# A streaming encoder step: the sample group's cache loads on ScalarE's queue, and small transfers merged

## The chip, the cores and the metric

The kernel runs on one core of a Trainium2 chip. The metric is the time of one execution on the device, in microseconds (us). Engines: PE is TensorE, DVE is VectorE, ACT is ScalarE, POOL is GpSimd, SP is SyncE, which computes nothing and only starts transfers. All transfers are carried by the core's 16 DMA engines.

## What is computed

One layer of an encoder, for two groups of requests that share the weights. The prompt group is one stream of 2048 new frames; the sample group is 8 streams of 16 new frames, each with 1024 cached frames. All numbers are float32. For both groups:

```
h = rmsnorm(x) * (1 + scale) + shift
z = h @ w_in                       # two conv parts, q, k, v, f
attention: s = q.k / 8 + cum_q - cum_k (causal), p = softmax(s), out = p.v
x = x + g1 * (concat(conv_module, attention) @ w_out)
x = x + g2 * ((silu(h2 @ w_gate) * (h2 @ w_up)) @ w_down)
```

`cum` is the running sum of the log forget values of a head. For a sample stream the keys, values and forget values are the cached ones followed by the new ones: `cache_k`, `cache_v` (8 streams, 1024 frames, 8 heads of 64) and `cache_logf`.

## The kernel before

The program goes through four stages: the projections (to about 625 us), the attention (625 to 1190 us), the output projection and the feed-forward part (the rest). The change lies in the attention.

**The prompt's attention** (`attention`, `attend`, from L804) is cut into 16 steps: a pair of heads `p` and a block `qb` of 512 queries. A step goes over tiles of 128 keys; for each tile and head PE makes a score tile (L1035, L1041, L1043) in one of three PSUM banks, ACT takes its exponential (L1045), PE multiplies by the values (L999). The row maxima come from products of their own (L952), which DVE reduces (L957), some 32 to 48 score tiles ahead; the maxima of a step are then written as a row, `mrow` (L970), into the query operand by eight transfers of 0.5 KB (L972). At the end of a step (`end_of_step`, L1062) the sums of the exponentials, four rows (two in a step with `qb` = 0) at partitions 0, 32, 64 and 96 of `sm`, are written to DRAM (L1080), loaded back in another shape (L1084), inverted on DVE (L1089), written (L1090), and loaded as a tile `aR` in which each of two rows is repeated over 64 partitions (L1094); DVE multiplies the result `zc` by it (L1097). These pieces are issued 3, 8, 13 and 20 score tiles after the end of the step (L1100).

**The sample's attention** runs as a background beside it (`background`, L878, woven in by `weave`). From `sample_setup` (L1135) on it holds the cached keys of a stream in two tiles `kc` of 1 MB (three buffers), the cached values in two tiles `vc` of 1 MB (two buffers), and the bias in a tile `S` (two buffers). `S` of stream `b` + 2 is loaded in the middle of `sample_values(b)` (L1305), the values of `b` + 1 after its products (L1315), and the keys three tiles ahead, after every second pair of key products (L1265). The bias stands in DRAM as four arrays `bias_d[j]` (rows: stream, head; 256 columns) and `biasn_d` (16 columns). Each row is repeated over the 16 queries of a stream, which makes 8 + 2 transfers for a stream (L1218, L1222), because head 2g + h stands in row 8s + 2g + h while the tile wants the halves h apart.

**The order of the work.** The engines take their instructions in a fixed order that the framework draws up at compile time, by the order of the program, priorities (the background's are 100 later) and a model of times. `late` and `after` add edges of order alone. All of these transfers are issued by SP, in its one order. The compiled program gives the transfers of the hardware queues eight semaphores in turn, and a transfer is held back by its issuing engine until the one eight places before it has landed.

```
1265  self.next_keys(2 * b + c + 3)
1266  yield
...
1315  self.next_values_of(b + 1)
1316  yield
```

Of the kernel before, what the change touches and what calls it, by code (L numbers as in the profile page):

```python
# [11 lines left out]
ALU = mybir.AluOpType  # L12
# [4 lines left out]
P = 128  # L17
# [3 lines left out]
NTP = T // P  # L21
NT = NTP + 1
TT = NT * P
NS = 8
QS = 16
H = 8
HD = 64
NP = H // 2
PAST = 1024
# [98 lines left out]
class Layer:  # L128
# [933 lines left out]
    def end_of_step(self, p, qb, zc, sums):  # L1062


        nc, wk = self.nc, self.awk
        parts = 2 if qb else 1
        r = slice(0, 64 * parts)
        sm = wk.tile([P, 512], F32, tag="sm", name="sm", bufs=1)
        self.last_exp = nc.scalar.copy(sm[r], sums[r])
        cat = self.cat_d[:, 4 + p, qb * 512:(qb + 1) * 512]  # L1070
        R = wk.tile([P, 512], F32, tag="R", name="aR", bufs=1)
        if (p, qb) == STEPS[-1]:
            spread = self.bank("ss", "R")
            nc.tensor.matmul(spread, self.four, sm, start=True, stop=True)
            nc.vector.reciprocal(R, spread)
            nc.vector.tensor_tensor(zc, zc, R, ALU.mult)
            nc.gpsimd.dma_start(cat, zc)
            return
        for i in range(2 * parts):
            nc.sync.dma_start(self.sum_d[p, qb, i:i + 1], sm[32 * i:32 * i + 1])  # L1080
        w = wk.tile([P, 2, 2, 4], F32, tag="inv", name="inv")

        def load():
            nc.sync.dma_start(w[:, 0:parts], self.sum_d[p, qb, 0:2 * parts].rearrange("(k h) (a c) -> a k h c", h=2, c=4))  # L1084

        def invert():
            if qb:
                self.after(nc.vector.tensor_tensor(w[:, 0], w[:, 0], w[:, 1], ALU.add), self.last_max)
            self.after(nc.vector.reciprocal(w[:, 0], w[:, 0]), self.last_max)  # L1089
            nc.sync.dma_start(self.inv_d[p, qb].rearrange("h (a c) -> a h c", c=4), w[:, 0])  # L1090

        def back():
            for h in range(2):
                nc.sync.dma_start(R[HD * h:HD * h + HD], self.inv_d[p, qb, h:h + 1].broadcast_to([HD, 512]))  # L1094

        def divide():
            self.after(nc.vector.tensor_tensor(zc, zc, R, ALU.mult), self.last_max)  # L1097
            nc.sync.dma_start(cat, zc)

        self.due += [(self.nscore + k, f) for k, f in ((3, load), (8, invert), (13, back), (20, divide))]  # L1100

    def late(self, op, last):
# [32 lines left out]
    def sample_setup(self, bank):  # L1135

        nc, a, sm = self.nc, self.a, self.smp
# [9 lines left out]
        sel = sm.tile([P, NS + QS], F32, name="sel")  # L1147
# [28 lines left out]
        for b in range(2):  # L1176
            pb = bank.rearrange("p (i k) -> p i k", i=4)
            for i in range(4):
# [4 lines left out]
                suf[:n, 4 * b:4 * b + 4].unsqueeze(2).broadcast_to([n, 4, P]), ALU.add)  # L1183
            yield
        lm = sm.tile([P, NS, H], F32, name="lm")
        nc.vector.tensor_tensor(lm, self.logf[:, NTP, :].unsqueeze(1).broadcast_to([P, NS, H]),
                                sel[:, 0:NS].unsqueeze(2).broadcast_to([P, NS, H]), ALU.mult)
        yield
        pn = bank[:, :QS]
        self.pe(pn[:n, :], lm.rearrange("p s h -> p (s h)"), sel[:, NS:], start=True, stop=True)  # L1190
# [10 lines left out]
        yield  # L1201
        yield

    def next_keys(self, i):

        if i < 2 * NS:
            kt = self.smc.tile([P, NP, 512], F32, tag="kc", name="kc", bufs=3)
            self.nc.sync.dma_start(kt, self.a["kcT"][i // 2, :, :, i % 2 * 512:i % 2 * 512 + 512])
            self.kc.append(kt)

    def next_bias(self, b):

        if b < NS:
            S = self.smp.tile([P, PAST + NP * QS], F32, tag="S", name="S", bufs=2)
            for j in range(4):
                for h in range(2):
                    rows = self.bias_d[j].rearrange("(s g h) k -> s h g k", s=NS, h=2)[b, h]
                    self.nc.sync.dma_start(S[32 * j + QS * h:32 * j + QS * h + QS, :PAST].rearrange("p (g k) -> p g k", g=NP),  # L1218
                                           rows.unsqueeze(0).broadcast_to([QS, NP, PAST // 4]))
            for h in range(2):  # L1220
                rows = self.biasn_d.rearrange("(s g h) k -> s h g k", s=NS, h=2)[b, h]
                self.nc.sync.dma_start(S[QS * h:QS * h + QS, PAST:].rearrange("p (g k) -> p g k", g=NP),  # L1222
                                       rows.unsqueeze(0).broadcast_to([QS, NP, QS]))
            kS = self.smp.tile([P, NP, QS], F32, tag="kS", name="kS", bufs=2)
            self.nc.sync.dma_start(kS, self.a["o_k"][:, :, T + b * QS:T + (b + 1) * QS].rearrange("g p t -> p g t"))
            self.S.append((S, kS))

    def next_values_of(self, b):

        if b < NS:  # L1230
            vs = []
            for c in range(2):
                v = self.smc.tile([P, 4, DC], F32, tag="vc", name="vc")
                self.nc.sync.dma_start(v, self.a["vc"][b, c * 512:c * 512 + 512].rearrange("(t p) e -> p t e", p=P))
                vs.append(v)
            vn = self.smp.tile([QS, DC], F32, tag="vn", name="vn")
            self.nc.sync.dma_start(vn, self.a["o_v"][T + b * QS:T + (b + 1) * QS, :])
            self.vs = vs, vn

    def sample_scores(self, b, bank):  # L1240

        S, kS = self.S.pop(0)
        Sc = S[:, :PAST].rearrange("p (g c k) -> p g c k", g=NP, c=2)
        Sn = S[:32, PAST:].rearrange("p (g k) -> p g k", g=NP)

        def q(g):
            return self.Qbd[:, g, b].rearrange("p h q -> p (h q)")

        for g in range(NP):
            self.pe(bank[:32, QS * g:QS * g + QS], q(g), kS[:, g, :], start=True, stop=True, tile_position=(0, 0))  # L1250
        yield
        self.dve("tensor_tensor", Sn, Sn, bank[:32, :NP * QS].rearrange("p (g k) -> p g k", g=NP), ALU.add)
        self.dve("tensor_tensor", Sn, Sn, self.maskS[:32].unsqueeze(1).broadcast_to([32, NP, QS]), ALU.add)
        yield
        for i in range(4):
            c, g0 = i // 2, i % 2 * 2
            if g0 == 0:
                kt = self.kc.pop(0)
            for g in (g0, g0 + 1):
                keys = kt[:, g].rearrange("p (t j k) -> p j t k", j=4, k=32)  # L1260
                for j in range(4):
                    self.pe(bank[32 * j:32 * j + 32, (g - g0) * P:(g - g0) * P + P].rearrange("p (t k) -> p t k", k=32), q(g), keys[:, j],
                            start=True, stop=True, tile_position=(0, 32 * j))
            if g0:
                self.next_keys(2 * b + c + 3)  # L1265
            yield
            s = Sc[:, g0:g0 + 2, c]
            self.dve("tensor_tensor", s, s, bank.rearrange("p (g k) -> p g k", g=2), ALU.add)
            yield
        self.scored = S, Sn  # L1270

    def sample_values(self, b, bank):

        sm = self.smp
        S, Sn = self.scored
# [13 lines left out]
        for g in range(NP):  # L1289
            s = S[:, g * PAST // 4:(g + 1) * PAST // 4]  # L1290
# [6 lines left out]
        parts = sm.tile([P, NP, 32], F32, tag="ob", name="parts")  # L1297
# [10 lines left out]
        for kt in range(9):  # L1308
            for g in range(NP):
                r = slice(32 * g, 32 * g + 32)  # L1310
                e = slice(g * P, (g + 1) * P)
                lhs, rhs = (ST[:, g, kt], vs[kt // 4][:, kt % 4, e]) if kt < 8 else (EnT[:QS, g], vn[:, e])
                self.pe(o[r, :], lhs, rhs, start=(kt == 0), stop=(kt == 8), tile_position=(0, 32 * g))
        self.pe(den, parts.rearrange("p g r -> p (g r)"), self.ones[:, 0:1], start=True, stop=True)
        self.next_values_of(b + 1)  # L1315
        yield
        ob = sm.tile([P, P], F32, tag="ob", name="ob")
        rd = sm.tile([P, 1], F32, tag="rd", name="rd")
        self.dve("reciprocal", rd, den)
# [466 lines left out]
def host_layout(inp):  # L1786
    import numpy as np

    inp = {n: np.asarray(v) for n, v in inp.items()}

    def c(x):
        return np.ascontiguousarray(x)
# [5 lines left out]
    def cols(w):  # L1798
# [21 lines left out]
        "w_down": c(inp["w_down"][0].reshape(NF // 2, 2, P, CB, P).transpose(1, 3, 2, 0, 4)),  # L1820
        "kcT": c(inp["cache_k"][0].reshape(NS, PAST, NP, P).transpose(0, 3, 2, 1)),
        "vc": c(inp["cache_v"][0].reshape(NS, PAST, DC)),
        "clfT": c(inp["cache_logf"][0].reshape(NS, 8, P, H).transpose(2, 1, 0, 3).reshape(P, 8, NS * H)),
        "ident": np.eye(P, dtype=np.float32),
    }
    i = np.arange(P)
# [8 lines left out]
    g = i % 32 // 8  # L1835
# [39 lines left out]
```

## Time and profile before

| | us |
|---|---|
| median of 3 runs (2797.23 to 2807.96) | 2799.87 |
| the profiled execution | 2804.1 |
| its span, first to last instruction | 2802.3 |
| PE busy in the span | 2716.7 |
| ACT busy in the span | 1235.4 |
| mean granted TensorE clock | 0.984 of full |

All durations below are of the profiled execution. A line such as L1045 is a line of the kernel. "SPq" is SP as the issuer of transfers, "DMA a<-b" is a transfer into a from b that something waited for, and an arrow `X <- Y` in a list of waits reads: X was idle until Y released it. PEclk is the granted clock of TensorE as a share of its full 2.4 GHz (0.50 is 1.2 GHz). A line L1105 is that of a helper that many of the sample's instructions go through, so the names of the tiles tell them apart.

### The profile page before, as it was taken

How to read it: one execution, taken by the hardware profiler on the slowest of the kernel's cores; microseconds unless marked ns; L12 is line 12 of the kernel's file. 1: busy time of each engine (PE TensorE's matmuls, PEld its weight loads, DVE VectorE, ACT ScalarE, POOL GpSimd, SP SyncE). 2: the span in 40 equal slices, each digit the busy share in tenths (PEclk: the TensorE clock that was granted, in tenths of full speed). 3: DMA queues.
4: the chain of work that ended last, by engine and by line, in shares of the span. 5: the costliest groups of instructions: out<-in, count | busy, mean ns of one | idle time of the engine just before them, and what ended most of it. 6: DMA issues, size and time to landing. Idle time of an engine off the chain costs nothing.

```text
span 2802.3 us, 49088 instructions
## 1 busy us (share of the span) xinstructions
PE 2716.7 (97%) x16930; PEld 2397.9 (86%) x16930; DVE 2029.7 (72%) x4132; ACT 1235.4 (44%) x2472; POOL 500.6 (18%) x686
## 2 busy tenths in 40 slices
PE   7999999999999989999999999999999999999999
PEld 6899988874445545498999999999999999999999
DVE  2798898974656566545397989877887778776765
ACT  4543323343444333444354446444554446555552
POOL 3454411223443221314201120000000000000000
PEclk9999999989999999999999999999999999999999
DMA  8863567673436577265576869866786769787873
GB/s 320 255 193 107 177 225 260 207 199 97 131 105 179 160 223 240 62 218 189 172 264 204 303 205 314 275 213 215 243 285 208 227 194 319 248 284 252 278 248 116
DMA packets 416978, 603.55 MB, mean 215 GB/s; under 512 B 65141, under 2 KB 280341, under 8 KB 414681
## 3 DMA queue, kind: packets, MB, share of 16 engines
q1 hardware_dynamic: 416520, 600.05, 67.0%
q8 instruction: 133, 2.18, 0.3%
q14 instruction: 117, 0.95, 0.1%
q0 software_dynamic: 208, 0.37, 0.0%
HBM read 426.00 MB, written 174.25 MB: 214 GB/s over the span
## 4 chain that ended last, share of the span: by engine, by line
PE 82%; DMA 8%; DVE 5%; issue 2%; ACT 1%; POOL 1%; SPq 1%; DVEq 0%; ACTq 0%; POOLq 0%
PE z L1665 45%; PE z L524 6%; PE acc L1353 5%; PE pv L999 4%; PE mx L952 3%; PE pa L332 3%; PE pvv L352 3%; PE pg L332 3%; PE s L1035 2%; PE lane L1105 2%; PE s L1041 2%; PE sm L988 1%; DMA wraw<-w_in 1%; DVE rW L1370 1%; DMA kc<-kcT 1%
## 5 line engine op out<-in xcount | busy, mean ns | idle before, releaser
L1665 PE MATMUL z<-rT,rW 128*128 128x360 f32 (+1 forms) x8316 | 1384.4, 328 | 3.9 <-ACT rW L1369 1.4
L1665 PEld LDWEIGHTS z<-rT,rW 128*128 128x128 f32 x8316 | 1380.1, 188 | 6.3 <-ACT rW L1369 2.4
L1369 ACT ACTIVATE rW<-rR 128x512 fp32r<-128x512 f32 x714 | 434.7, 616 | 388.7 <-PE z L1665 277.0
L1370 DVE TENSOR_TENSOR rW<-rR,rW 128x512 fp32r<-128x512 f32 x714 | 477.3, 673 | 160.3 <-ACT rW L1369 155.8
L712 DVE SCALAR_TENSOR_TENSOR cv<-cu,cpar,cv 128x384 f32<-128x384 f32 x580 | 311.7, 615 | 2.5 <-ACT cv L710 2.4
L1045 ACT ACTIVATE e<-s 128x512 f32<-128x512 f32 (+3 forms) x320 | 166.4, 532 | 284.2 <-PE s L1041 163.9
L957 DVE TENSOR_REDUCE M<-mx 128x1 f32<-128x512 f32 (+2 forms) x320 | 190.2, 605 | 133.7 <-PE mx L952 106.4
L524 PE MATMUL z<-hqx,wqh 128*128 128x384 f32 (+1 forms) x768 | 197.4, 333 | 1.3 <-DVE logf L359 1.3
L1369 ACT ACTIVATE rT<-traw 128x360 fp32r<-128x360 f32 (+1 forms) x315 | 149.8, 501 | 81.8 <-DMA traw<-gt_d 50.8
L1370 DVE TENSOR_TENSOR rT<-traw,rT 128x360 fp32r<-128x360 f32 (+1 forms) x315 | 158.0, 531 | 34.0 <-ACT rT L1369 33.3
L952 PE MATMUL mx<-K,Q 96*128 96x512 f32 (+2 forms) x320 | 142.4, 458 | 21.1 <-DVE M L957 12.6
L999 PE MATMUL pv<-e,V 128*64 128x512 f32 (+3 forms) x640 | 157.1, 558 | 0.0
L952 PEld LDWEIGHTS mx<-K,Q 96*128 96x128 f32 x320 | 62.8, 199 | 109.9 <-DVE M L957 57.2
L524 PEld LDWEIGHTS z<-hqx,wqh 128*128 128x128 f32 x768 | 136.1, 188 | 17.6 <-issue 12.4
L1353 PE MATMUL acc<-ch,woh 128*128 128x360 f32 (+1 forms) x384 | 127.1, 333 | 6.3 <-DVE xo L1361 3.9
L1593 DVE TENSOR_TENSOR rR<-rR 128x512 f32<-128x512 f32 (+1 forms) x136 | 92.0, 696 | 56.6 <-DMA rR<-w_down 50.5
L1035 PE MATMUL s<-Q,K 128*128 128x512 f32 (+3 forms) x320 | 131.0, 409 | 0.3 <-ACT e L1045 0.2
L1353 PE MATMUL acc<-ch,wol 128*128 128x360 f32 (+1 forms) x384 | 126.7, 330 | 0.0
L524 PE MATMUL z<-hqx,wql 128*128 128x384 f32 (+1 forms) x384 | 126.5, 329 | 0.0
L1041 PE MATMUL s<-Q,K 128*128 128x512 f32 (+3 forms) x320 | 120.3, 376 | 4.6 <-DMA Q<-mrow 4.6
L1353 PE MATMUL acc<-cl,woh 128*128 128x360 f32 (+1 forms) x384 | 122.9, 330 | 0.7 <-DVE cl L1370 0.6
L1011 POOL TENSOR_TENSOR sums<-e,sums 128x512 f32<-128x512 f32 x72 | 97.4, 1353 | 100.2 <-ACT e L1045 96.9
(317 smaller groups left out, 3728.5 us busy)
## 6 DMA issues: line engine op xcount, KB each, us to landing
rR<-sup_d SPq DMA_DIRECT2D x176, 256.0 KB
rR<-w_gate SPq DMA_DIRECT2D x132, 256.0 KB
traw<-gt_d SPq DMA_DIRECT2D x154, 180.0 KB
rR<-w_down SPq DMA_DIRECT2D x104, 256.0 KB
rR<-sdn_d SPq DMA_DIRECT2D x96, 256.0 KB
rR<-w_up SPq DMA_DIRECT2D x88, 256.0 KB
sup_d<-rR SPq DMA_DIRECT2D x88, 256.0 KB
wa<-w_ada SPq DMA_DIRECT2D x16, 1024.0 KB
```

The lines of the kernel that those rows point to most:

```text
L332: nc.tensor.matmul(pz[:, :n], w[:, m], x[:, :n], start=(c == 0 and k == 0), stop=(c == CB - 1 and k == 2))
L524: nc.tensor.matmul(z[:, :n], w[:, m], x[:, :n], start=(c == 0 and k == 0), stop=(c == CB - 1 and k == 2))
L712: self.pin(nc.vector.scalar_tensor_tensor(dst, src, w, acc[i], ALU.mult, ALU.add))
L952: self.mx.append(nc.tensor.matmul(mx[:, :w], Q2[0:AUX, h, j * P:(j + 1) * P], K2[kb][0:AUX, h, :w], start=True, stop=not diag))
L957: self.last_max = nc.vector.tensor_reduce(M[:, i, kb:kb + 1], mx[:, :w], AX.X, ALU.max)
L999: product = nc.tensor.matmul(z[0][HD * h:HD * h + HD, off:], V[kt // 4][:, kt % 4, HD * h:HD * h + HD], es[h][:, off:], start=(kt == 0), s ...
L1035: first = nc.tensor.matmul(s[:, off:], K1[kb][:, h, sl], Q1[:, h, off:], start=True, stop=False)
L1041: self.last_s = nc.tensor.matmul(s[:, off:], K2[kb][:, h, sl], Q2[:, h, off:], start=False, stop=not diag)
L1353: self.nc.tensor.matmul(z[:, :n], w[:, m], y, start=(first and i == 0 and k == 0), stop=(last and i == len(terms) - 1 and k == 2))
L1369: copy = self.nc.scalar.activation(hi, raw, AF.Copy)
L1370: engine.tensor_tensor(lo, raw, f32(hi), ALU.subtract)
L1665: nc.tensor.matmul(z, W[:, x, m], t[:, y, :w], start=(k == 0 and i == 0), stop=(k == n - 1 and i == 2))
```

## The change

The loads of `kc` and `vc` go to ScalarE's queue, each with an edge of order behind the latest exponential. The places where the keys and the values are asked for move behind the next `yield`. The four sum rows of a step leave in one transfer, the two repeated rows of `aR` come in one, and the bias of a stream comes in five, for which the head order of the cached forget values (in the host's layout) and of the new ones (`lm`, now two instructions) becomes h, g.

```
-        for i in range(2 * parts):
-            nc.sync.dma_start(self.sum_d[p, qb, i:i + 1], sm[32 * i:32 * i + 1])
+        nc.sync.dma_start(self.sum_d[p, qb, 0:2 * parts], sm[0:64 * parts:32])
...
-            for h in range(2):
-                nc.sync.dma_start(R[HD * h:HD * h + HD], self.inv_d[p, qb, h:h + 1].broadcast_to([HD, 512]))
+            nc.sync.dma_start(R, self.inv_d[p, qb].unsqueeze(1).broadcast_to([2, HD, 512]))
...
-        nc.vector.tensor_tensor(lm, self.logf[:, NTP, :].unsqueeze(1).broadcast_to([P, NS, H]),
-                                sel[:, 0:NS].unsqueeze(2).broadcast_to([P, NS, H]), ALU.mult)
+        for h in range(2):
+            nc.vector.tensor_tensor(lm[:, :, NP * h:NP * h + NP], self.logf[:, NTP, h::2].unsqueeze(1).broadcast_to([P, NS, NP]),
+                                    sel[:, 0:NS].unsqueeze(2).broadcast_to([P, NS, NP]), ALU.mult)
...
+    def bulk(self, *args):
+        return self.late(self.nc.scalar.dma_start, self.last_piece)(*args)
...
-            self.nc.sync.dma_start(kt, self.a["kcT"][i // 2, :, :, i % 2 * 512:i % 2 * 512 + 512])
+            self.bulk(kt, self.a["kcT"][i // 2, :, :, i % 2 * 512:i % 2 * 512 + 512])
...
             for j in range(4):
-                for h in range(2):
-                    rows = self.bias_d[j].rearrange("(s g h) k -> s h g k", s=NS, h=2)[b, h]
-                    self.nc.sync.dma_start(S[32 * j + QS * h:32 * j + QS * h + QS, :PAST].rearrange("p (g k) -> p g k", g=NP),
-                                           rows.unsqueeze(0).broadcast_to([QS, NP, PAST // 4]))
-            for h in range(2):
-                rows = self.biasn_d.rearrange("(s g h) k -> s h g k", s=NS, h=2)[b, h]
-                self.nc.sync.dma_start(S[QS * h:QS * h + QS, PAST:].rearrange("p (g k) -> p g k", g=NP),
-                                       rows.unsqueeze(0).broadcast_to([QS, NP, QS]))
+                rows = self.bias_d[j].rearrange("(s h g) k -> s h (g k)", s=NS, h=2)[b]
+                self.nc.sync.dma_start(S[32 * j:32 * j + 32, :PAST], rows.unsqueeze(1).broadcast_to([2, QS, PAST]))
+            rows = self.biasn_d.rearrange("(s h g) k -> s h (g k)", s=NS, h=2)[b]
+            self.nc.sync.dma_start(S[:32, PAST:], rows.unsqueeze(1).broadcast_to([2, QS, NP * QS]))
...
-                self.nc.sync.dma_start(v, self.a["vc"][b, c * 512:c * 512 + 512].rearrange("(t p) e -> p t e", p=P))
+                self.bulk(v, self.a["vc"][b, c * 512:c * 512 + 512].rearrange("(t p) e -> p t e", p=P))
...
+            yield
             if g0:
                 self.next_keys(2 * b + c + 3)
-            yield
...
+        yield
         self.next_values_of(b + 1)
-        yield
...
-        "clfT": c(inp["cache_logf"][0].reshape(NS, 8, P, H).transpose(2, 1, 0, 3).reshape(P, 8, NS * H)),
+        "clfT": c(inp["cache_logf"][0].reshape(NS, 8, P, NP, 2).transpose(2, 1, 0, 4, 3).reshape(P, 8, NS * H)),
```

## Rows read from the trace of the kernel before

**Rows 1.** The page's first part: busy time, share of the span, instructions.
```profile
PE 2716.7 (97%) x16930; PEld 2397.9 (86%) x16930; DVE 2029.7 (72%) x4132; ACT 1235.4 (44%) x2472; POOL 500.6 (18%) x686
```

**Rows 2.** Stretches: length, busy PE PEld DVE ACT POOL, PEclk, DMA share, GB/s.
```profile
625.00:885.00 260.00, 252.23 (x1233) 129.51 (x1231) 153.75 (x281) 116.93 (x258) 112.28 (x123) 0.97 0.39 113
...
965.00:1125.00 160.00, 147.06 (x1448) 83.56 (x1444) 105.39 (x265) 57.85 (x143) 28.78 (x26) 0.95 0.74 227
...
1195.00:2803.00 1608.00, 1586.86 (x9548) 1580.56 (x9547) 1191.37 (x2318) 768.65 (x1496) 101.39 (x91) 0.99 0.73 238
```

**Rows 3.** Who PE waited for, 625 to 1190 us: total, times, longest.
```profile
PE s L1041 <- DMA Q<-mrow: 4.6, 1, 4.6
PE mx L952 <- DVE rsx L1105: 5.5, 1, 5.5
PE lane L1105 <- DVE S L1105: 3.4, 1, 3.4
PE mx L952 <- DMA Q<-q_d: 2.0, 1, 2.0
```

**Rows 4.** Stretches at half clock, and the 2 us gap before the first.
```profile
901.50:903.50 2.00, 0.03 (x1) 0.00 (x0) 0.00 (x0) 0.00 (x0) 0.00 (x0) 1.00 1.07 353
905.30:908.70 3.40, 3.40 (x11) 1.03 (x7) 0.84 (x3) 0.00 (x0) 0.00 (x0) 0.50 1.06 260
...
936.00:942.80 6.80, 5.75 (x29) 2.40 (x31) 2.88 (x8) 0.60 (x1) 0.00 (x0) 0.50 0.59 149
...
987.20:994.00 6.80, 3.94 (x11) 2.38 (x12) 2.68 (x7) 1.04 (x2) 0.00 (x0) 0.50 0.87 195
...
1048.70:1058.90 10.20, 8.43 (x33) 3.86 (x34) 5.15 (x12) 1.48 (x4) 0.40 (x1) 0.50 0.69 189
```

**Rows 5.** DVE's waits on transfers, 640 to 1190 us: total, times, longest.
```profile
DVE zc L1097 <- DMA aR<-inv_d: 10.7, 3, 7.1
DVE S L1105 <- DMA S<-biasn_d: 4.6, 1, 4.6
```

**Rows 6.** Timeline of SP: start, us, line, transfer, count.
```profile
964.66 5.00 SPq L1218 DMA_DIRECT2D S<-bias_d  x8
...
973.69 6.66 SPq L972 DMA_DIRECT2D Q<-mrow  x6
...
1025.98 11.47 SPq L972 DMA_DIRECT2D Q<-mrow  x8
```

**Rows 7.** Who SP's queue waited for, 880 to 1130 us.
```profile
SPq L972 <- DMA vc<-vc: 9.9, 6, 2.3
SPq L1208 <- PE s L1043: 5.5, 1, 5.5
SPq L1208 <- PE mx L952: 5.0, 2, 4.7
SPq L1234 <- PE lane L1105: 3.8, 5, 1.5
SPq L1208 <- DMA kc<-kcT: 3.8, 2, 2.5
```

**Rows 8.** Issues of the touched transfers: count, ns min/median/max, first and last start.
```profile
L1208 SPq DMA_DIRECT2D kc<-kcT x16: 560/604/628, 889.2 to 1107.1; - x16
L1234 SPq DMA_DIRECT2D vc<-vc x16: 372/451/2364, 895.5 to 1126.0; - x16
L1094 SPq DMA_DIRECT2D aR<-inv_d x30: 451/590/1357, 668.2 to 1166.0; - x30
L1218 SPq DMA_DIRECT2D S<-bias_d x64: 302/424/1807, 928.0 to 1104.0; - x64
```

**Rows 9.** Sizes of two of the merged transfers: count, KB each.
```profile
S<-bias_d SPq DMA_DIRECT2D x64, 64.0 KB
aR<-inv_d SPq DMA_DIRECT2D x30, 128.0 KB
```

**Rows 10.** DVE's timeline: the first use of stream 2's bias tile.
```profile
979.83 0.20 DVE L1105 TENSOR_TENSOR S<-S,lane 32x64 f32<-32x64 f32 x1
```

## The prediction

> **What bounds the kernel now.** The page's first part comes first: PE is busy 97% of the span [rows 1]. The second view is the table of stretches: from 1195 us to the end PE is busy 1586.86 of 1608 us [rows 2], so 57% of the span is PE's own work, which the change doesn't touch. What can move lies in the attention. From 625 to 885 us PE is busy 252.23 of 260 us and the DMA engines 0.39; from 965 to 1125 us, in the middle of the sample's streams, PE is busy 147.06 of 160 us, its clock is 0.95, and the DMA engines are at 0.74 [rows 2]. So the sample's loads make the stretch with the idle time.
>
> The third view, PE's waits in the attention, names four idle gaps with a transfer behind them: 2.0 us for a query load, 3.4 us for DVE at the bias tile `S`, 4.6 us for `mrow`, 5.5 us behind DVE at L1105 [rows 3], 15.5 us together. Behind two of them stands a DVE that waits itself: 4.6 us for `biasn_d`, and 7.1 us for `aR`, which is the longest of three waits of 10.7 us in all [rows 5]. The fourth view shows what each gap drags along. Soon after each begins the clock is at 0.50, for 3.4, 6.8, 6.8 and 10.2 us [rows 4]: 27.2 us at 1.2 GHz, in which half, 13.6 us, is lost. The four gaps cost 29.1 us with their clock.
>
> Why the transfers are late is read from SP's timeline. Ten transfers of a stream's bias take SP over 5 us, then come the two `vc` and a `kc`, and then six `mrow` transfers of 0.5 KB take 6.66 us; eight of them take 11.47 us later on [rows 6]. SP's waits say what held them: 9.9 us for `vc` to land, in 6 waits [rows 7]. That is the rule of eight semaphores: a 0.5 KB transfer is held until a 1 MB one has landed. SP also stands 5.5 + 5.0 + 3.8 us with a `kc` or `vc` in hand whose buffer PE hasn't freed, and 3.8 us for an earlier `kc` [rows 7], 18.1 us in which all that follows in its order waits too.
>
> **The loads on ScalarE's queue.** 16 `kc` issues of 604 ns and 16 `vc` issues of 451 ns [rows 8] leave SP and come to ACT: 9.7 + 7.2 = 16.9 us. ACT is busy 57.85 of 160 us in that stretch [rows 2], and three score banks stand between PE and the exponentials, so I cost the issues at nothing; if that cover is gone, each delays an exponential by some 0.6 us. The added wait is worse than the issue: behind a load that waits on ACT stand the exponentials, behind them PE's scores. Its bounds are nothing and the 18.1 us that SP waited. I take 1 us, because the requests move behind a `yield`, when PE's products are mostly done. What is gained: the gaps at the query load, at `mrow` and at `aR` all come from small transfers behind large ones. They go, 2.0 + 4.6 + 5.5 = 12.1 us, with their clock, (3.4 + 6.8 + 10.2) / 2 = 10.2 us: **-22.3 us**. The gap at `S` I leave in place: its own transfers end it. The extra `lm` instruction on DVE, once, costs some 0.2 us by the nearest small DVE row [rows 10], in the stage before the first stream, beside PE's own work: nothing.
>
> **The merged transfers.** On SP 37 `sum_d`, 15 `aR` and 40 bias issues fall away, 0.4 to 0.6 us for one of the last two kinds [rows 8]; SP's issue time is on no path once the waits are gone, so this is counted within the 22.3. But the shape changes. Today a bias load names 16 rows outermost, an `aR` load 64. Afterwards both name two rows outermost, each repeated. No row shows on how many engines such a transfer runs. One end: all 16, as long as now or a little shorter, no cost. Other end: the transfer can be cut only between the two rows, and two engines carry it all. With every engine busy 353 GB/s moved [rows 4], 22 GB/s for one. A stream's bias is 8 x 64 KB [rows 9], 524 KB, 262 KB on each of two engines: 11.9 us instead of 1.5. An `aR` of 2 x 128 KB [rows 9] takes 131 KB / 22 = 6.0 us instead of 0.7. As neither end has a row near it, I take a middle: the two-engine length, counted only where it comes past its need; both ends stay in the range.
>
> Is it felt? `S` of stream 2 is issued from 964.66 us [rows 6] and first used at 979.83 [rows 10], 15.2 us later. Alone, 0.4 + 11.9 us fits with 2.9 to spare. The `vc` pair and a `kc` of the other queue, 3 MB or 8.9 us on each engine, take turns with it: late by up to 6.0. I take half, 3.0 us for each of six streams: 18 us of DVE waits. Before, a DVE wait of 4.6 us cost PE 3.4 and one of 7.1 cost 5.5 [rows 3, 5], three quarters: 13.5 us. Such gaps of 2.2 us are as short as the shortest that the clock followed, so I charge half of the rate of before (13.6 / 15.5), 6.0 us. Together **+19.5 us**. `aR` lands 5.3 us later in 15 steps. In twelve of them DVE didn't wait before [rows 5], and the 7 score tiles between issue and use hide it; two further waits of 3 us are left, **+4.5 us** on PE.
>
> The Trainium skill ("DMA: Bandwidth & Descriptors", section "Rules for kernel authors") speaks against this edit: an outermost dimension of a size c below 16 confines the whole transfer to at most c engines. By it the two-engine end holds and the sum stands as above; without it the +24.0 us fall away and the time is that of the first rival. No row of this trace shows it.
>
> **The sum.** -22.3 + 1 + 19.5 + 4.5 = +2.7 us on the profiled execution's 2804.1 us (span 2802.3 and 1.8 around it), 2806.8. That execution is 4.2 us above the median of the runs, 2799.87; against the median it is 2802.6, about **2803 us**. A measurement of this kernel tells some 0.5% from no change: 14 us.
>
> **The rivals.**
> *Faster: the merged transfers are not felt.* They run wide, or land in time. Then the three gaps go, and the one at `S` too (3.4 us and 3.4 of clock): -29.1, about 2771; with the ACT waits, 2771 to 2780, say 2776. For it: the DMA engines are at 0.39 and 0.74, not full [rows 2]. Against it: the new shape.
> *Slower: two engines become the bound.* In the six streams from 965 to 1125 us each has 26.7 us. On each of the two engines it would need 11.9 us for the bias, 6.0 for one step's `aR`, 11.9 for its share of 4.2 MB of keys and values, and 3.1 for the rest (227 GB/s over 160 us [rows 2] is 36.3 MB, less 29.8 of those three): 32.9 us. Six streams need 197 us for 160. Of the 37 us over, the 15.2 us that `S` is ahead are forgiven: +22 us, and the old gaps drown in it: 2822. The point from which it decides is a two-engine load above 26.7 + 15.2 / 6 = 29.2 us a stream. For it: the sum itself. Against it: 22 GB/s is a mixed rate, and longer rows may go faster.
> *Slower: ACT takes SP's place as the one that waits.* The 18.1 us of waits and half of the 16.9 us of issues reach PE, 26.5 us, and the clock falls with the waits (0.88 x 18.1 = 16): -22.3 + 42.5 = +20, 2820. The semaphores that the two queues share speak for it, since a load on ACT can then wait for a transfer that SP hasn't landed; ACT's idle time against it [rows 2].
>
> **How the numbers follow.** The forecast has 0.40: it is the partial case between the first two rivals. The faster rival has 0.26, the two-engine bound 0.22, ACT's waits 0.12. That the change doesn't do what it says I can't see. The forecast is within 0.5% (2786 to 2814), the first rival below, the other two above: faster 0.26, same 0.40, slower 0.34. The range reaches to the first rival's lower end, 2771, and past the two slow ones by the uncertainty of the engine's rate (10% of 197 us, half of it inside): 2770 to 2834.
>
> **What would show it.** Right: no SP wait for `vc` or `kc` in front of `mrow`; the 4.6 us gap at L1041 and the 5.5 us one gone; `S` and `aR` waits on DVE more often, of some 3 us; PE busy in 965 to 1125 about as before. First rival: no DVE wait on `S` or `aR` over 1 us, and the clock at 1.00 throughout. Second: DVE waits on `S`, `aR` and SP waits on `S` of 5 us and more, the last product with `vc` some 20 us later, and in between a low GB/s at a high wait. Third: ACT's list names DMA landings or PE's key products ahead of `e`, and PE waits at L1035 for `e`. Wrong altogether: a change of more than 5 us outside 885 to 1195 us.

## The result, and the profile after

| | before | after |
|---|---|---|
| median (us) | 2803.91, 4 runs (2797.23 to 2812.22) | 2876.72, 4 runs (2872.33 to 2878.63) |
| ratio | | 1.026, 95% interval 1.0241 to 1.0278 |
| span of the profiled execution | 2802.3 | 2873.9 |
| mean granted clock | 0.984 | 0.976 |

The change makes the kernel slower by 2.6%, 73 us. The forecast was 2803 us, its range ended at 2834: the prediction was wrong. All that follows asks which of its steps failed.

In the changed kernel some lines have moved by up to two: the sample's helper is L1103, the bias loads are L1220 and L1222, `aR` is loaded at L1092 and used at L1095. First the stretches of the changed kernel (length; busy PE, PEld, DVE, ACT, POOL; PEclk, DMA share, GB/s):

```profile
625.00:885.00 260.00, 251.00 (x1224) 126.05 (x1223) 146.11 (x280) 113.87 (x253) 110.86 (x121) 0.98 0.39 112
965.00:1125.00 160.00, 122.55 (x1076) 65.26 (x1078) 82.31 (x196) 44.74 (x114) 22.79 (x21) 0.85 0.57 169
1195.00:1270.00 75.00, 68.35 (x377) 35.16 (x376) 34.67 (x59) 32.68 (x67) 17.83 (x14) 0.95 0.18 56
1270.00:2874.00 1604.00, 1581.57 (x9517) 1575.92 (x9515) 1190.30 (x2313) 765.52 (x1491) 101.03 (x90) 0.99 0.73 238
```

The last 1604 us hold the work that the last 1608 us held before, and 625 to 885 us is unchanged [rows 2]. So the loss lies between 885 and 1270 us, in the sample's streams. From 965 to 1125 us PE lost 24.5 us of busy time, its clock fell from 0.95 to 0.85, and the DMA engines, which have the same bytes to bring in all, fell from 0.74 to 0.57 [rows 2]: transfers became late while most engines had less to do. The whole stretch, before (to 1195 us) and after (to 1270 us), holds about the same work in 75 us more:

```profile
885.00:1195.00 310.00, 287.07 (x2302) 154.43 (x2301) 187.95 (x423) 116.19 (x266) 60.98 (x52) 0.96 0.61 181
...
885.00:1270.00 385.00, 310.12 (x2313) 163.60 (x2312) 189.39 (x420) 117.48 (x269) 59.60 (x51) 0.89 0.50 148
```

PE's idle time grew from 22.9 to 74.9 us, 52 us, and the same products took 23 us longer at the lower clock.

The pace of the streams is read from one instruction that each stream has once, the mask added to its new scores. In the view of the tile `S`, the times of the first and the last of the eight, before:

```profile
L1105 DVE TENSOR_TENSOR S<-S,maskS x8: 201/208/1140, 937.0 to 1117.7; 32x64 f32<-32x64 f32 x8
```

and after:

```profile
L1103 DVE TENSOR_TENSOR S<-S,maskS x8: 201/207/993, 937.4 to 1177.2; 32x64 f32<-32x64 f32 x8
```

The first stream starts at the same time. Seven intervals take 239.8 us instead of 180.7: 34.3 us a stream instead of 25.8, 59 us more where the span grew by 72. The pace alone is not the loss, though: below, e13 has 28.4 us a stream and is the fastest kernel of all. What is lost is the time in which PE stands idle meanwhile, and the clock after it.

Who waited for whom in the changed kernel, 620 to 1280 us:

```profile
PE s L1035 <- ACT e L1045: 37.1, 9, 12.6
...
DVE S L1103 <- DMA S<-biasn_d: 26.4, 5, 10.6
...
DVE zc L1095 <- DMA aR<-inv_d: 23.1, 5, 8.9
PE mx L952 <- DVE M L957: 22.9, 11, 12.2
...
PE lane L1103 <- DVE S L1103: 13.8, 4, 7.7
...
ACT e L1045 <- DMA S<-bias_d: 12.4, 1, 12.4
...
ACT e L1045 <- DMA kS<-o_k: 10.9, 1, 10.9
...
ACT e L1045 <- DMA Q<-mrow: 9.7, 1, 9.7
ACT e L1045 <- DMA vn<-o_v: 9.1, 1, 9.1
```

DVE's waits for `S` and `aR` grew from 4.6 and 10.7 us [rows 5] to 26.4 and 23.1. An exponential reads no `kS`, `mrow` or `vn`: ACT's waits for them are those of a `kc` or `vc` load in front of it. The timeline of ACT shows one such place:

```profile
1006.65 1.08 ACT L1045 ACTIVATE e<-s 128x512 f32<-128x512 f32 x2 [10.23 <-PE mx L952]
1022.29 0.55 ACTq L1103 DMA_DIRECT2D kc<-kcT  x1
1022.94 1.08 ACT L1045 ACTIVATE e<-s 128x512 f32<-128x512 f32 x2 [15.21 <-issue]
```

The `kc` load is issued at 1022.29 us, and ACT had stood idle for 15.21 us before the exponential behind it. By the trace the load's semaphore is that of a bias transfer that SP issued at 1006.64 us and that landed at 1022.23. SP stands still as well. Its longest waits for the bias in the same stretch:

```profile
SPq L972 <- DMA S<-bias_d: 24.1, 6, 5.6
...
SPq L869 <- DMA S<-bias_d: 14.1, 4, 4.1
...
SPq L1089 <- DMA S<-bias_d: 9.4, 2, 4.9
...
SPq L925 <- DMA S<-bias_d: 8.5, 1, 8.5
```

How long a bias takes is in two views, SP's timeline

```profile
969.08 2.56 SPq L1220 DMA_DIRECT2D S<-bias_d  x4
971.68 0.58 SPq L1222 DMA_DIRECT2D S<-biasn_d  x1
```

and the chain of waits (start, us, step):

```profile
971.68 18.09 DMA S<-biasn_d
...
1152.62 23.96 DMA S<-biasn_d
```

The fifth transfer of the first has 8 KB and lands 18.09 us after its issue, 20.7 us after the first of the five. 0.53 MB in 20.7 us are 26 GB/s, where every engine together moved 353 [rows 4].

Why it takes so long stands in a part of the trace that no view above prints: a transfer's semaphore is raised in steps, and the time of each is kept. Of the transfers that SP and ACT issue from 885 to 1230 us, the wide ones have sixteen steps (three `K` loads twelve). A bias transfer of the changed kernel has three, one at 1.0 us after its issue (the median) and two when its data has come; the merged sums of four rows have five, and the eight-row bias of e9 below has nine. So behind that first step there are as many as rows outermost, and I read each as one engine's share. The two engines of the merged transfers delay the others too. Before, no step of the 296 transfers with sixteen came more than 2 us behind the one ahead of it. In the changed kernel that happens in 65 of 149, and in 63 of them just the last two steps are late. A `vc` load has its fourteenth step 6.9 us after its issue and its last 7.2 us behind that, where before it was 7.5 and 0.24 us (medians of 16). So the wide transfers wait for their pieces on two engines, and that it is always two says that the narrow ones share the same pair.

### The profile page after: what moved, and what is told of

The parts are those of the page before. It is cut to its first block, busy times and chain, and to the rows that moved or that the text cites. A ratio compares the mean times of both kernels' runs of the same rounds, so it can differ in the third digit from the quotient of the medians.

```text
span 2873.9 us, 48942 instructions
## 1 busy us (share of the span) xinstructions
PE 2736.0 (95%) x16930; PEld 2399.8 (84%) x16930; DVE 2027.3 (71%) x4133; ACT 1233.1 (43%) x2472; POOL 497.9 (17%) x686
## 4 chain that ended last, share of the span: by engine, by line
PE 77%; DMA 14%; DVE 4%; issue 2%; ACT 2%; SPq 1%; POOL 1%; ACTq 0%; DVEq 0%; POOLq 0%
PE z L1664 46%; PE z L524 6%; PE acc L1352 4%; PE pv L999 3%; PE pa L332 3%; PE pg L332 3%; PE mx L952 2%; PE s L1035 2%; PE pvv L352 2%; PE lane L1103 2%; PE s L1041 1%; DMA S<-biasn_d 1%; DMA S<-bias_d 1%; DMA aR<-inv_d 1%; DMA cat_d<-cy 1%
## 5 line engine op out<-in xcount | busy, mean ns | idle before, releaser
L1035 PE MATMUL s<-Q,K 128*128 128x512 f32 (+3 forms) x320 | 134.5, 420 | 37.1 <-ACT e L1045 37.1
L1035 PEld LDWEIGHTS s<-Q,K 128*128 128x128 f32 x320 | 64.0, 200 | 82.6 <-ACT e L1045 57.6
```

The lines of the kernel that those rows point to most:

```text
L1035: first = nc.tensor.matmul(s[:, off:], K1[kb][:, h, sl], Q1[:, h, off:], start=True, stop=False)
```

## The experiments

Two theories to begin with. **Shape:** the merged bias and inverses are carried by few engines, land late, and everything else follows. **Queue:** the loads on ACT are held, and the exponentials behind them. The ratios are to the kernel before, timed beside each run, with their 95% intervals.

### The two halves of the change

**e1_act_only** has only the loads on ACT and the moved requests, **e2_merge_only** only the merges.

```
-            self.nc.sync.dma_start(kt, ...)        # e1: kc, and vc alike; e2 leaves them on SP
+            self.bulk(kt, ...)
...                                                    # e1: the requests behind the next yield
```

> The kernel before with one part of the change: the loads of kc and vc on ScalarE's queue and the requests behind the next yield; no transfer is merged. Theory 'shape' (the merged bias and inverse transfers land late because few engines carry them; everything else follows from that): within 0.7% of before, 2785 to 2820 us, S and aR in no wait of DVE above 5 us. Theory 'queue' (the loads on ACT are held by their buffers and by the semaphores shared with SP, and the exponentials behind them): most of the 73 us is here, 2840 us or more, and PE waits for e at L1035 some 30 us in all, as in the changed kernel (37.1 us). A mixture of halves would give about 2835.

> The kernel before with the other part: sums, inverses and bias in merged transfers (and the order of heads that this needs), the loads of kc and vc left on SP. Theory 'shape': most of the 73 us is here, 2845 to 2890 us; DVE waits for S and aR some 40 us or more in all, SP waits for S, and PE waits for DVE at S and mx. Theory 'queue': 2785 to 2820 us, and DVE's waits for S and aR stay below 15 us in all (before: 4.6 and 10.7).

e1: 2792.75 us, 0.9979 (0.9966 to 0.9992). e2: 2869.42 us, 1.0246 (1.023 to 1.0261). The merges are the loss; the loads on ACT gain a little by themselves, and beside the merges nothing that shows (2876.72 us with them, 2869.42 without). The gain of 6 us is smaller than the 22.3 us summed, in good part for a reason seen in e1's own trace, the timeline of ACT

```profile
908.05 0.57 ACTq L1105 DMA_DIRECT2D kc<-kcT  x1
908.72 0.94 ACT L1045 ACTIVATE e<-s 128x128 f32<-128x128 f32 x3 [9.82 <-DMA sum_d<-sm]
```

its waits, and the stretch that came after (columns as above):

```profile
PE s L1035 <- ACT e L1045: 6.6, 1, 6.6
```

```profile
904.46:918.11 13.65, 9.06 (x37) 4.51 (x37) 1.68 (x3) 3.29 (x7) 1.27 (x1) 0.50 0.81 238
```

A `kc` load on ACT was held for a transfer of SP's. The bracket names the last of several, `sum_d`; the semaphore of the load itself was that of a `K` load, issued at 898.40 us and landed at 907.89. PE lost 6.6 us, and half of the 9.06 us in which it was busy at half clock: 11.1 us at one place.

### Wide again, piece by piece

**e3_S_wide** is the changed kernel with the bias in 8 + 2 transfers; **e4_all_wide** has the inverses in two as well.

```
-                rows = ...rearrange("(s h g) k -> s h (g k)", ...)[b]
-                self.nc.sync.dma_start(S[32 * j:32 * j + 32, :PAST], rows.unsqueeze(1).broadcast_to([2, QS, PAST]))
+                for h in range(2):
+                    rows = ...rearrange("(s h g) k -> s h (g k)", ...)[b, h]
+                    self.nc.sync.dma_start(S[32 * j + QS * h:32 * j + QS * h + QS, :PAST], rows.unsqueeze(0).broadcast_to([QS, PAST]))
...                                                    # the small ones by halves too; e4: aR as before
```

> The changed kernel with the bias of a stream in 8 + 2 transfers again, 16 rows outermost, now with rows of 4 KB; the merged sums and inverses and the loads on ACT stay. Theory 'shape', if the bias is the larger part of it: 2790 to 2830 us, the wait of DVE for biasn_d (26.4 us) under 6, and ACT's e no longer behind S. Theory 'queue': the time stays within 20 us of the changed kernel's 2877.

> As the run before, and the inverses in two transfers again (64 rows outermost): of the merges only that of the sums is left, and the loads are on ACT. Theory 'shape': 2780 to 2815 us, some 10 us under the run before, as the wait for aR (23.1 us in the changed kernel) falls below 8. Theory 'queue': 2850 us or more. If the inverses' transfer is harmless: the same as the run before within 5 us.

e3: 2812.34 us, 1.0037 (1.0025 to 1.0049). e4: 2796.53 us, 0.9986 (0.9975 to 0.9996). 64 us of the 73 come back with the bias, another 16 with the inverses (with the loads on ACT in all three). The queue theory falls.

**e5_cut8** and **e9_one_S** ask whether it is the outermost dimension or the size and number of the transfers.

```
# e5: two rows outermost, cut by columns into 8 of 64 KB
+                for c in range(2):
+                    cols = slice(PAST // 2 * c, PAST // 2 * c + PAST // 2)
+                    self.nc.sync.dma_start(S[32 * j:32 * j + 32, cols], rows[:, cols].unsqueeze(1).broadcast_to([2, QS, PAST // 2]))
...                                                    # the two small ones: 16 rows outermost
# e9: bias_d laid out as [stream, 4, 2, PAST], one transfer of 512 KB with eight rows outermost
+            self.nc.sync.dma_start(S[:, :PAST], self.bias_d[b].rearrange("j h k -> (j h) k").unsqueeze(1).broadcast_to([8, QS, PAST]))
```

> The changed kernel, but a stream's bias in 8 + 2 transfers instead of 4 + 1: each of the four is cut in two by its columns, so that it still names two rows outermost (32 rows of 2 KB, 64 KB each); the two small ones name 16. It has as many transfers, of the same size, as the run e3_S_wide (2812 us), which differs only in cutting by halves of the heads. Theory 'few engines' (what counts is the outermost dimension): about the changed kernel, 2855 to 2890 us, DVE's wait for S above 15 us. Rival 'large transfers' (what counts is that a transfer is twice as large and there are fewer of them): 2805 to 2825 us, as e3_S_wide.

> The changed kernel with the bias laid out in DRAM as eight rows of 4 KB for a stream (part of the frames, half of the heads), so that one transfer of 512 KB with eight rows outermost fills the 128 partitions; the small one for the new frames keeps two rows outermost. That is two transfers for a stream, fewer than the change has, and four times as large. Theory 'few engines': eight engines carry it, the length falls to a quarter, and the time is that of the run with eight transfers of 16 rows (2812 us), within 10 us: 2802 to 2822. Rival 'fewer and larger transfers are slow': 2870 us or more.

e5: 2864.15 us, 1.0241 (1.0226 to 1.0257): as many transfers as e3, of the same 64 KB, and 52 us slower. e9: 2818.33 us, 1.007 (1.0054 to 1.0086): the fewest and largest transfers (only the 8 KB one keeps two rows), and 6 us from e3. What counts is how many rows stand outermost: 2 are slow, 8 and 16 are not. So the first end of the bounds, all 16 engines, is excluded, and the other, two engines, agrees with the steps and the 26 GB/s above. This agrees with the Trainium skill ("DMA: Bandwidth & Descriptors", section "Rules for kernel authors"), which the prediction had weighed.

### Each merge alone

> The kernel before with the bias merged (five transfers, two rows outermost) and nothing else. From the runs so far: both merges with the loads on SP cost 69 us; S should carry most of it, 2845 to 2870 us. If S and aR only hurt together (they share the same two engines): under 2825 us.

> The kernel before with the inverses' two transfers merged into one (two rows outermost) and nothing else. With the loads on ACT this merge cost 16 us (2812 against 2797). Expected here 2805 to 2818 us, DVE's wait for aR at 15 us or more instead of 10.7. If it only hurts beside the merged bias or on ACT: 2795 to 2805.

> The kernel before with the four sum rows of a step in one transfer (four rows outermost, two in a step with qb = 0) and nothing else: the last part of the change not yet run alone. If a transfer of few rows only costs by its length, which is 8 KB here: 2795 to 2802 us, the same as before. If the held semaphores or the later inverse count: 2803 to 2810.

The edits are those of the change, one at a time:

```
# e7:  the bias hunk, with lm and clfT     # e8:  the R hunk
# e15
-        for i in range(2 * parts):
-            nc.sync.dma_start(self.sum_d[p, qb, i:i + 1], sm[32 * i:32 * i + 1])
+        nc.sync.dma_start(self.sum_d[p, qb, 0:2 * parts], sm[0:64 * parts:32])
```

e7: 2841.89 us, 1.0162 (1.0145 to 1.0179), 45 us, some 3 us below what was expected. e8: 2815.44 us, 1.007 (1.0052 to 1.0088), 18.5 us by the medians. e15: 2802.06 us, 1.001 (0.9996 to 1.0023), no difference: a narrow transfer of 8 KB costs nothing that shows. The ratios of e1, e7, e8 and e15 add up to 1.0221, 62 us; the whole change is 73, which is hardly beyond the intervals. Clearer is the bias: it costs 45 us alone, and 64 us beside the rest of the change (e3 against the changed kernel). In e7, which leaves the loads on SP and `aR` wide, the streams' pace is 216.4 / 7 = 30.9 us:

```profile
L1105 DVE TENSOR_TENSOR S<-S,maskS x8: 201/203/291, 935.2 to 1151.6; 32x64 f32<-32x64 f32 x8
```

and its waits, 620 to 1280 us, have

```profile
DVE S L1105 <- DMA S<-biasn_d: 21.9, 4, 11.2
...
PE lane L1105 <- DVE S L1105: 16.1, 6, 6.7
```

PE's waits behind `S` are 16.1 us here, where they were 3.4 [rows 3]: much less than the 45 us.

### By which way a late transfer costs time

**e6_S_pool** issues the merged bias from GpSimd's queue, **e12_loads_pool** the keys and values; otherwise they are the changed kernel.

```
-                self.nc.sync.dma_start(S[32 * j:32 * j + 32, :PAST], ...)     # e6, and the small one
+                self.nc.gpsimd.dma_start(S[32 * j:32 * j + 32, :PAST], ...)
...
-        return self.late(self.nc.scalar.dma_start, self.last_piece)(*args)     # e12
+        return self.late(self.nc.gpsimd.dma_start, self.last_piece)(*args)
```

> The changed kernel with the merged bias transfers issued by GpSimd's queue instead of SP's; their shape stays. It tells two ways apart by which a late S costs time. If mainly DVE's own wait for S and PE behind it does (way 'S itself'): 2850 to 2885 us, with DVE's wait for S at 20 us or more. If mainly the transfers held on SP and ACT until S has landed do (way 'held transfers': 24.1 us of SP's waits at L972 are for S): 2800 to 2830 us, SP and ACT wait for S no longer, mrow and aR are in time.

> The changed kernel with the loads of kc and vc on GpSimd's queue instead of ScalarE's; the merged transfers stay as they are, on SP. It asks what of the loss comes through ACT: in the changed kernel its e stands behind loads held for S, mrow, kS and vn. If late S and aR reach PE through DVE and SP alone: within 8 us of the changed kernel (2869 to 2885), and of the merges alone with the loads on SP (2869). If ACT's held loads are a route of their own: 2835 to 2860 us, and ACT's waits of 9 to 15 us for transfers are gone.

e6: 2812.84 us, 1.0048 (1.003 to 1.0067), as if the bias were wide. But it doesn't tell its two ways apart, because on this queue the same transfers were not late. The view of the tile `S` gives their issues, and the time from issue to landing:

```profile
L1220 POOL DMA_DIRECT2D S<-bias_d x32: 582/599/717, 922.1 to 1122.7; - x32
...
DMA to landing us min/median/max: 4.7/7.1/19.4
```

The median is 7.1 us. In the changed kernel the same 40 transfers from SP's queue have a median of 14.1 by their last steps; the 18.09 and 23.96 us above are late ones. And where a sixteen-step transfer of SP or ACT has its last two steps late by over 2 us in 63 cases of 149 in the changed kernel, it does in 16 of 191 here. The Trainium skill ("DMA: Bandwidth & Descriptors", section "Why a DMA increments its semaphore by 16 and not by 1") says that such a transfer goes to the lowest-numbered of the engines when SP or ACT issues it, and to the next ones in turn when GpSimd does. That would put every narrow transfer of SP's on one pair and let GpSimd's run side by side. The times and the steps agree, but nothing here names the engines.

e12: 2872.79 us, 1.0267 (1.0252 to 1.0283), the same as the changed kernel. ACT's waits for `S`, `kS`, `mrow` and `vn` are gone, and others are longer, as its waits show:

```profile
DVE S L1103 <- DMA S<-biasn_d: 48.1, 6, 11.5
...
PE lane L1103 <- DVE S L1103: 38.8, 6, 9.2
...
PE s L1035 <- ACT e L1045: 4.4, 1, 4.4
```

PE's wait for `e` fell from 37.1 to 4.4 us, its wait behind `S` rose from 13.8 to 38.8, and nothing was gained; the streams' pace is 34.3 us, as in the changed kernel:

```profile
L1103 DVE TENSOR_TENSOR S<-S,maskS x8: 201/202/211, 943.8 to 1183.9; 32x64 f32<-32x64 f32 x8
```

On GpSimd the loads have waits of their own, so this run alone would not settle it. But with the merges the time is within 8 us wherever the loads are issued: ACT (2876.72), SP (e2, 2869.42) or GpSimd (2872.79). So ACT is no route of its own: whoever waits, the slow transfers set the pace.

**e14_spare** adds the slow transfers without making `S` slow: the kernel before, and behind a stream's bias loads four transfers of the change's shape into a DRAM array that nothing reads.

```
+            for j in range(4):
+                rows = self.bias_d[j].rearrange("(s h r) k -> s h (r k)", s=NS, h=2)[b]
+                self.nc.sync.dma_start(self.spare_d[b, j], rows.unsqueeze(1).broadcast_to([2, QS, PAST]))
```

> The kernel before, its bias loads as they were (16 rows outermost), and behind them on SP, for each stream, four transfers of the change's shape (two rows outermost, 128 KB) from the bias into DRAM that nobody reads. The two engines carry the same load as in the run e7_S_only (2842 us) and SP's semaphores are held as long, but S itself comes over all engines. Theory 'late S' (DVE waits for S, PE behind it): at most 2815 us. Theory 'load and held transfers' (two busy engines and held semaphores delay everything, S among it): 2830 us or more. Between 2815 and 2830 both have a share.

2851.56 us, 1.0188 (1.0171 to 1.0204), 51 us for transfers that nobody waits for as data. DVE's wait for `S` is about as short as before [rows 5], and the waits for the prompt's keys, queries and inverses are long (here the helper is L1106, and other lines stand one later than before):

```profile
DVE zc L1098 <- DMA aR<-inv_d: 29.6, 4, 9.4
...
PE mx L953 <- DMA K<-k_d: 14.4, 1, 14.4
...
PE mx L953 <- DMA Q<-q_d: 11.6, 2, 9.4
...
DVE S L1106 <- DMA S<-biasn_d: 5.6, 2, 5.2
```

SP's queue in this run, 885 to 1260 us:

```profile
SPq L1219 <- DMA spare_d<-bias_d: 20.7, 11, 2.2
...
SPq L973 <- DMA spare_d<-bias_d: 13.1, 8, 2.0
```

and the streams' pace, 233.8 / 7 = 33.4 us:

```profile
L1106 DVE TENSOR_TENSOR S<-S,maskS x8: 203/213/1074, 931.1 to 1164.9; 32x64 f32<-32x64 f32 x8
```

So `S` itself need not be late. Narrow transfers on SP's queue are enough: SP is held until they have landed, and what it issues behind them comes late. The other way is seen as well: in 43 of 249 transfers of sixteen steps just the last two came over 2 us late, `aR` by up to 7.7 us and a `mrow` by 11.7. How the 51 us divide between the two, no run separates. Nor was the same load tried in wide transfers: the 4 MB more and the 32 further issues on SP have a share in the 51 us that is not known. More lead for `S` (a third buffer) was not tried.

### Towards a better version

**e10_best** is e1 with the bias of e9, **e13_S_pool_best** is e1 with the merged bias on GpSimd's queue; both leave sums and inverses in separate transfers. **e16_all_pool** is the whole change, with bias and inverses on GpSimd's queue.

```
-            nc.sync.dma_start(R, self.inv_d[p, qb].unsqueeze(1).broadcast_to([2, HD, 512]))     # e16, and S as in e6
+            nc.gpsimd.dma_start(R, self.inv_d[p, qb].unsqueeze(1).broadcast_to([2, HD, 512]))
```

> The kernel before with the loads of kc and vc on ScalarE's queue and a stream's bias in one transfer of eight rows and a small one; sums and inverses stay in separate transfers. It joins the part of the change that gained (2792.75 us alone, 0.9979 of before) with a merge that leaves the bias on eight engines. If fewer issues on SP are worth anything once nothing lands late: 2780 to 2791 us. If not: 2790 to 2797. Above 2800 the eight writes and the shape cost time still.

> The kernel before with the loads of kc and vc on ScalarE's queue and the merged bias (four transfers and a small one, two rows outermost) on GpSimd's queue, where the run e6_S_pool showed it landing in 7.1 us (median); sums and inverses in separate transfers. From e6_S_pool (2813) less what the merged inverses cost (16): 2790 to 2800 us. If an emptier SP is worth more than that: 2780 to 2790.

> The changed kernel with the merged bias and the merged inverses both issued by GpSimd's queue: every edit of the change stays, only the issuing engine of two kinds of transfers differs. If the few engines of SP's transfers are the whole loss: 2780 to 2800 us, about as the run e13_S_pool_best (2784.5). If GpSimd issues the inverses too late (its own products and sums stand in front of them): 2800 to 2815, with DVE's wait for aR at 15 us or more.

e10: 2797.39 us, 0.9998 (0.9987 to 1.001): a merge that keeps eight engines gains nothing over e1 (0.9979), and whether it costs a few us isn't settled, as the intervals just overlap; it lies at the end of what was expected without a gain (2790 to 2797). e13: 2784.52 us, 0.9962 (0.9948 to 0.9977): the fastest of all kernels here, 14 us below before by the medians and some 90 below the change, with 28.4 us a stream (927.2 to 1126.0 us); the intervals of e13 and e1 overlap, so what the merge adds to the loads on ACT isn't settled. e16: 2819.11 us, 1.0072 (1.0048 to 1.0095), which misses the expectation of 2780 to 2800 and lies 4 us above the other, in which GpSimd issues the inverses late. GpSimd also does the running sums of the prompt's exponentials, and its waits, 625 to 1250 us, show what the inverses do there:

```profile
POOL aR L1092 <- DMA inv_d<-inv: 59.4, 7, 20.5
```

An issue of `aR` waits on GpSimd for the row written just before, 59.4 us in all, and everything behind it in that engine's order waits too. It is the same mistake as on SP, one engine further.

## Why the prediction was wrong

The forecast was the partial case: two engines carry the bias, and this is felt a little. Two engines, the direction of each term and the place (885 to 1195 us) were right; three sizes were not, and behind the largest a step was missing.

- **Loads on ACT, -22.3 and +1.** Measured together: 0.9979, 6 us gained. The term that was mis-sized is the added wait: not 1 us but 11.1, clock included, at one place, within the bounds of 0 to 18.1. The cover of three score banks didn't last while ACT stood idle for 9.82 us behind a held load. The gain was priced a little high as well: in the three stretches at half clock that it counts PE was busy for 15.8 of 20.4 us [rows 4], so they cost 7.9 us and not 10.2. With both put right the sum is -9 us, which agrees with the 6 measured within the interval.
- **Merged bias, +19.5.** Measured alone: 45 us. The wait itself was nearly right: "3.0 us for each of six streams" makes 18 us of DVE waits, and e7 has 21.9. The step that fails is the next one, that these waits are all that a narrow bias costs. The prediction let the keys and values delay the bias on the two engines, but not the bias the keys, values and `mrow`: a `vc` load's last two steps come 7.5 us behind its fourteenth in e7, 0.24 us before. And the rule of eight semaphores stood in the first part of the prediction, but it was used for what the change removes (`mrow` behind `vc`) and not for what it adds: everything that SP issues behind a narrow bias. e14 shows the two together at up to 51 us with `S` itself in time.
- **Merged inverses, +4.5.** Measured alone: 0.7%, about 19 us. The transfer was late by about the 5.3 us forecast: its median to landing is 8.9 us in e8 and 3.2 before, 5.7 us more. "The 7 score tiles between issue and use hide it" fails: in e8 DVE waits for `aR` six times, 26.7 us in all, where it was three times and 10.7 [rows 5].
- **Merged sums, 0.** Measured: 1.001 with an interval that holds 1. Right.
- **The sum.** It adds the terms as if they were independent. The bias alone costs 45 us, beside the rest of the change 64.
- **The second rival** (two engines become the bound, 0.22) had the mechanism nearest to the result. Its demand of 32.9 us a stream is close to the measured pace of 34.3, which may be in part luck: where GpSimd issues the bias, the pace is still 30.1 us in e6 and 28.4 in e13. Its price of 22 us was too low: it counted six streams against 160 us and took off 15.2 us for the lead of `S`. In the changed kernel all seven intervals are longer, 59 us together, and what PE pays between 885 us and the end of the streams is 52 us of idle time and 23 us of lower clock.
- **The range** ended at 2834, above the second rival's price. Even the prices of both slow rivals together, 22 and 20 us, would have ended at 2842.

Of the signs named beforehand, those of the second rival came: waits of up to 10.6 us for `S` and 8.9 for `aR` on DVE, SP waits for `S` of up to 8.5, low GB/s in between. Those of the third came too (DMA landings ahead of `e`, PE waiting at L1035), but e12 shows that they were where the delay surfaced, not what caused it.

## What to carry to other kernels

Count a transfer's outermost rows before merging it: 2 rows of the bias cost 45 us, 8 or 16 next to nothing, in fewer transfers or in more, and 8 KB in four rows cost nothing that shows. A slow transfer's price is not only the wait of its reader; look at what its queue issues behind it, how many semaphores that queue has, and which other transfers have a piece on the same engines. For a load that comes back every stream, compare the demand on its few engines with the stream's time: a lead is there once, and a surplus comes in every stream.

## What was not expected of the hardware

The same two-row transfers that landed 14.1 us after issue from SP's queue (the median) took 7.1 us from GpSimd's, and the kernel 64 us less (2812.84 against 2876.72). And transfers that nobody reads slowed the kernel by 51 us while the DMA engines' mean share in the streams was 0.59 from 965 to 1125 us, where it had been 0.74 [rows 2]: a share averaged over 16 engines says little when two of them carry a queue. The times of a transfer's single steps say more: fourteen on time and two late.
